# The head of a hybrid attention and state-space block, reordered

## The chip, the cores and the metric

One core of a Trainium2 chip runs the whole program in one launch. The metric is the device time of that launch in microseconds (us), lower is better. The engines of the core are TensorE (PE in the profile, with its weight loads PEld), VectorE (DVE), ScalarE (ACT), GpSimd (POOL) and SyncE (SP), which only issues transfers here. Each takes its instructions strictly in the order of its own queue and waits there for what the next instruction needs.

## What is computed

The reference is a streaming-encoder block on 1040 rows (16 meta tokens and 1024 tokens) of width 1024, all in float32. Cut to what this case needs:

```
xn   = rmsnorm(concat(meta, x), g)
q, k, v, f, u, gates = split(xn @ w_in)
y_a  = forgetting_attention(q, k, v, f) @ w_attn_out
z    = gelu(s5(u))                 # diagonal state-space model, 32 groups x 64 states
zg   = z @ w_glu
y_s  = zg[:, :1024] * sigmoid(zg[:, 1024:])
g    = sigmoid(gates)
h    = h + (g[:, :1024] * y_a + g[:, 1024:] * y_s) @ w_o
h    = h + (silu(gate) * val) @ w_down    # val, gate = causal conv of rmsnorm(h) @ w_up
out  = rmsnorm(h)[16:]

s5:  lam_bar = exp(lam * dt), dt = exp(log_dt), b_bar = (lam_bar - 1) / lam * b
     state_t = lam_bar * state_(t-1) + b_bar u_t;  y_t = Re(c state_t) + d u_t
```

## The kernel before

Activations are held by features: xhi and xlo are two tiles [128, 8, 1040] whose sum is the normalised input, a rounded part and the rest. Weights are split the same way (whi, wlo). A product of such pairs is three matmuls for each slice of 128 features (L146, L147, L148 in `dense_steps`): hi by hi, hi by lo, lo by hi.

The head, which is what the change touches, does the following.

- The meta tile (`xm`, 16 rows) and eight token tiles (`xt`, 128 rows) are loaded. `norm_rows` squares one on ScalarE (L161), turns the sum into mean plus epsilon on VectorE (`vr`, L163), takes the power -0.5 on GpSimd (`rs`, L165) and scales the tile by it and by the gain `g1B` on VectorE (L166).
- `to_feature` transposes the scaled tile in two halves of four 128x128 pieces on TensorE (L175), copies each half to xhi on ScalarE (L177) and writes the rest to xlo on VectorE (L126).
- `u_weights(m)` splits the weights of column chunk m (0 to 3) of the state-space input: a copy on ScalarE (L281) and a subtraction on VectorE (L126). `u_proj(0)` multiplies chunks 0 and 1 and `u_proj(2)` chunks 2 and 3, each over three blocks of 272, 384 and 384 rows (24 matmuls a block and chunk), and writes u to DRAM.
- `ssm(...)` builds the state-space model. Its first step, the discretisation, is a long row of small VectorE operations on tiles of 128x32 (`sm`), from log dt and lambda to the powers of lam_bar. `tables(q)` then makes Gm, Kt, Vm and Wi for a quarter of the groups (TensorE at L1495 and L1515), and `chain(q)` the recurrence (L1532, L1572).
- Between those, `gate_chunk(i)` for i = 8 to 15 multiplies the second half of the gates. Its weights come by `wchunk` with `act` and `adds` set: a load on GpSimd's queue (L130), a rounded copy on ScalarE (L134), the negative raw weights on ScalarE (L138), and a second, accumulating load that adds the raw weights' bits (L139), which leaves raw minus rounded in `wlo`.
- After the gates come the first pair of q and k (`project_qk`), the forget gate, and `load_z` with the glu.

The buffers `raw`, `whi` and `wlo` exist twice, so a new weight chunk waits until the matmuls of the last but one are done. In the head the same `raw` slots hold two of the four u weight tiles.

The order within each engine's queue comes from a scheduler that simulates the program; `after(a, b)` adds a rule of order by hand that a comes after b. In what follows names with a number (sm_155, whi_951) are single buffers of that name.

## Time and profile before

| what | value |
|---|---|
| time, median of three runs (lowest to highest) | 1498.87 us (1498.07 to 1501.14) |
| the profiled execution, its own time | 1501.19 us |
| span of that execution, first to last instruction | 1499.4 us |
| mean granted clock of TensorE | 0.992 |
| busy: PE, DVE, ACT, POOL | 1452.1, 1067.2, 678.4, 656.9 us |
| chain that ended last, by engine | PE 78%, DVE 12%, DMA 4%, issue 3% |
| transfers | 187.81 MB, mean 125 GB/s |

Rows of the profile are read so: a group or an instruction shows its line, engine and operation, then written tile and read tiles with partitions x elements, then its time, and in brackets how long the engine idled before it and what released it. A row of a stretch shows the stretch, its length, the busy time and number of instructions of each engine, the granted clock of TensorE (1.00 is full), the share of the transfer engines and GB/s. A row of waits shows who waited for what: us in total, how often, longest. The chain of waits is the work that ended last, followed back from release to release.

### The profile page before, as it was taken

The page shows a single profiled execution, that of the slowest core. Times are in us where ns is not written, and L with a number is a line of the kernel's source. Part 1 is how long each engine was busy: PE and PEld are TensorE (multiplying, and loading weights), DVE is VectorE, ACT ScalarE, POOL GpSimd, SP SyncE. Part 2 cuts the span into 40 slices and gives each one's busy share as a digit, 9 for nine tenths or more (in the row PEclk, how much of TensorE's full clock was granted, in tenths as well). Part 3 has the DMA queues.
Part 4 walks back from the last instruction along what each step waited for, and adds up shares of the span by engine and source line. Part 5 has one row for each costly group of instructions (what it writes and reads, how often), then busy time and mean ns, then how long its engine had stood idle before and what let it go on. Part 6 is the DMA issues. An engine that isn't in the chain of part 4 may idle for free.

```text
span 1499.4 us, 26213 instructions
## 1 busy us (share of the span) xinstructions
PE 1452.1 (97%) x9637; PEld 1364.1 (91%) x9637; DVE 1067.2 (71%) x2259; ACT 678.4 (45%) x1321; POOL 656.9 (44%) x743
## 2 busy tenths in 40 slices
PE   5999999999999999999999999999999999989997
PEld 4999999998999999999778999999999999768886
DVE  7989568862657676656255988887787776688785
ACT  6255565532646565532033534444444445444433
POOL 2010004750655556525010235555544326689765
PEclk9999999999999999999999999999999999999998
DMA  5365553550121212157241226776643215864413
GB/s 214 87 151 150 128 142 100 166 160 30 33 79 40 79 32 83 43 185 269 84 158 68 71 86 168 198 193 186 158 115 96 74 60 177 320 214 125 143 36 113
DMA packets 82837, 187.81 MB, mean 125 GB/s; under 512 B 13610, under 2 KB 26554, under 8 KB 82356
## 3 DMA queue, kind: packets, MB, share of 16 engines
q1 hardware_dynamic: 68212, 155.56, 31.8%
q0 software_dynamic: 8704, 19.98, 7.4%
q10 hardware_dynamic: 5792, 10.60, 1.9%
q8 instruction: 76, 1.25, 0.4%
q14 instruction: 53, 0.43, 0.1%
HBM read 146.98 MB, written 61.00 MB: 139 GB/s over the span
## 4 chain that ended last, share of the span: by engine, by line
PE 78%; DVE 12%; DMA 4%; issue 3%; ACT 2%; POOL 1%; SPq 0%; POOLq 0%; DVEq 0%; ACTq 0%
PE mm L148 5%; PE mm L146 5%; PE mm L147 5%; PE sp L203 4%; PE sp L204 4%; PE sp L205 4%; PE tp L203 3%; PE tp L204 3%; PE tp L205 3%; PE tp L685 2%; PE mm L203 2%; PE mm L205 2%; PE mm L204 2%; PE po L707 2%; PE po L706 2%
## 5 line engine op out<-in xcount | busy, mean ns | idle before, releaser
L148 PE MATMUL mm<-xhi,wlo 128*128 128x342 f32 (+2 forms) x584 | 191.0, 328 | 2.3 <-DMA wlo<-in_w_g_dram 2.3
L146 PE MATMUL mm<-xhi,whi 128*128 128x342 f32 (+2 forms) x584 | 191.9, 329 | 1.0 <-DVE q L126 1.0
L147 PE MATMUL mm<-xlo,whi 128*128 128x342 f32 (+2 forms) x584 | 190.8, 327 | 1.4 <-DVE xlo L126 1.4
L148 PEld LDWEIGHTS mm<-xhi,wlo 128*128 128x128 f32 x584 | 111.5, 191 | 3.1 <-DMA wlo<-in_w_g_dram 2.5
L146 PEld LDWEIGHTS mm<-xhi,whi 128*128 128x128 f32 x584 | 111.8, 192 | 2.1 <-PE sp L643 0.8
L147 PEld LDWEIGHTS mm<-xlo,whi 128*128 128x128 f32 x584 | 111.8, 191 | 2.1 <-DVE xlo L126 1.7
L126 DVE TENSOR_TENSOR sw<-sf,sw 128x512 fp32r<-128x512 f32 x76 | 72.5, 955 | 48.6 <-ACT sw L937 48.5
L968 POOL TENSOR_TENSOR ov<-ov,og 128x1024 f32<-128x1024 f32 x21 | 51.4, 2449 | 120.6 <-ACT og L967 117.7
L937 ACT CAST sw<-sf 128x512 fp32r<-128x512 f32 x76 | 47.4, 624 | 113.4 <-POOL sf L945 86.0
L945 POOL TENSOR_TENSOR sf<-raw,sf 128x512 f32<-128x512 f32 x38 | 64.9, 1709 | 69.1 <-DVE sw L126 68.8
L205 PE MATMUL mm<-xhi,sw 128*128 128x256 f32 (+1 forms) x304 | 85.5, 281 | 0.0
L203 PE MATMUL mm<-xhi,sw 128*128 128x256 f32 (+1 forms) x304 | 85.4, 281 | 0.1
L204 PE MATMUL mm<-xlo,sw 128*128 128x256 f32 (+1 forms) x304 | 85.2, 280 | 0.0
L692 ACT CAST th<-tp 128x256 fp32r<-128x256 f32 (+3 forms) x120 | 56.1, 472 | 61.6 <-PE tp L685 28.6
L126 DVE TENSOR_TENSOR tl<-tp,th 128x256 fp32r<-128x256 f32 (+3 forms) x120 | 65.2, 547 | 26.1 <-ACT th L692 24.7
L937 ACT CAST sw<-raw 128x512 fp32r<-128x512 f32 x69 | 42.4, 620 | 83.3 <-DMA raw<-in_w_up_dram 36.4
L657 POOL TENSOR_SCALAR pt<-pt,nm 128x144 f32<-128x144 f32 (+4 forms) x72 | 50.9, 708 | 52.3 <-DVE nm L656 51.0
L945 POOL TENSOR_TENSOR sf<-raw 128x512 f32<-128x512 f32 x38 | 50.5, 1329 | 52.0 <-DMA raw<-in_w_up_dram 24.8
L1034 DVE SCALAR_TENSOR_TENSOR ov<-hv,cwt,ov 128x1024 f32<-128x1024 f32 x38 | 72.9, 1919 | 0.4 <-ACT ov L1032 0.4
L655 ACT ACTIVATE pt<-pt,nm 128x144 f32<-128x144 f32 (+4 forms) x72 | 52.9, 735 | 26.2 <-DVE nm L654 25.8
L648 DVE CUSTOM_DVE_ANT_0 pt<-sp,fb 128x328 f32<-128x328 f32 (+8 forms) x112 | 46.4, 430 | 20.6 <-PE sp L643 12.3
L165 POOL TENSOR_TENSOR rs<-vr,nhalf 128x1 f32<-128x1 f32 (+2 forms) x18 | 10.5, 592 | 109.5 <-PE mm L889 52.4
(606 smaller groups left out, 5417.9 us busy)
## 6 DMA issues: line engine op xcount, KB each, us to landing
raw<-in_w_up_dram SPq DMA_DIRECT2D x44, 512.0 KB, 3.7
t_d<-in_w_dn_dram POOLq DMA_DIRECT2D x44, 256.0 KB, 6.9
ar<-a_d SPq DMA_DIRECT2D x44, 256.0 KB, 4.9
wr<-t_d SPq DMA_DIRECT2D x44, 256.0 KB, 3.1
a_d<-ov SPq DMA_DIRECT2D x21, 512.0 KB, 2.6
wr<-in_w_dn_dram SPq DMA_DIRECT2D x33, 256.0 KB, 3.5
t_d<-in_w_dn_dram SPq DMA_DIRECT2D x22, 256.0 KB, 4.4
t_d<-t_d SPq DMA_DIRECT2D x22, 256.0 KB, 4.5
```

The source lines that it names most:

```text
L126: return eng.tensor_tensor(out_, src, hi.bitcast(F), ALU.subtract)
L146: yield PE.matmul(ps, whi[:, i, :], ahi[:, i], start=(i == 0), stop=False)
L147: yield PE.matmul(ps, whi[:, i, :], alo[:, i], start=False, stop=False)
L148: yield PE.matmul(ps, wlo[:, i, :], ahi[:, i], start=False, stop=(i == k - 1))
L203: PE.matmul(ps, a[0][:, i], bh, start=(i == 0 and not joins), stop=False, skip_group_check=True)
L204: PE.matmul(ps, a[0][:, i], bl, start=False, stop=False, skip_group_check=True)
L205: PE.matmul(ps, a[1][:, i], bh, start=False, stop=(i == kh - 1), skip_group_check=True)
L655: S.activation(pt[:n, :kc], pt[:n, :kc], AF.Exp, bias=nm[:n, 1:2], scale=0.125, accum_out=nm[:n, 2:3])
L692: S.copy(th[:kn, z:tw], tp[:kn, z:tw])
L937: S.copy(hi, src)
L945: sums.append(GP.tensor_tensor(f_, a, b, op))
L1034: V.scalar_tensor_tensor(out=o, in0=h_[:, j:SEQ + j], scalar=cwc(j, m), in1=o, op0=ALU.mult, op1=ALU.add)
```

## The change

It does ten things, nine of them in the head.

1. `u_weights` takes its weights by column chunks: the array `w_u` is laid out in blocks, one 512 KB tile for each chunk m instead of one for each two slices of features. A chunk is split with two copies and two subtractions of 128x512 instead of four and four of 128x256. Chunk 0 is split ahead of token tile 2 and chunk 1 ahead of token tile 3 (tile 0 is the meta tile) instead of before all tiles.
2. The loads of SP's queue stand in another order: `g1B` first (it was on ScalarE's queue), and the four u chunks between the token tiles.
3. The discretisation starts behind the scaling of the fifth tile (`scales[4]`) instead of before the tiles.
4. It is shorter: polynomials take one operation a step instead of two (`horner`), complex products work on both parts in one tile (`cmul`), and the powers are built as unit numbers E and radii rp.
5. From token tile 3 on, the squares of a tile come after the xhi copies of the tile two before (`done[i - 2]`), where only tile 3 came after the copies of the tiles before it.
6. 20 transposes of the identity stand at the head of TensorE's queue (L299).
7. `u_proj(2)` goes through all blocks of chunk 2 and then all of chunk 3; before, the two alternated by block, as they still do in `u_proj(0)`.
8. `wchunk` loads on GpSimd's queue where `act` is set, which now includes the first q and k weights.
9. Four of the 32 z loads (m = 3, odd g) go to GpSimd's queue.
10. `norm_rows` returns its scaling instruction as well, for point 3.

The diff, with the discretisation cut to its core:

```diff
-        (GP if adds else SY).dma_start(raw, src)
+        (GP if act else SY).dma_start(raw, src)
...
-    uraw = [wp.tile([P, 2, SW], F, tag="raw", name="uraw") for _ in range(2)]
-    uraw += [sp.tile([P, 2, SW], F, tag="Tm", name="uraw", bufs=2) for _ in range(2)]
+    uraw = [wp.tile([P, KD, P], F, tag="raw", name="uraw") for _ in range(2)]
+    uraw += [sp.tile([P, KD, P], F, tag="Tm", name="uraw", bufs=2) for _ in range(2)]
...
-        for j, raw in enumerate(uraw):
-            src, sl = raw[:, :, P * m:P * m + P], slice(2 * j, 2 * j + 2)
-            S.copy(hi[:, sl], src)
-            split_lo(V, lo[:, sl], src, hi[:, sl])
+        for j in range(2):
+            sl = slice(4 * j, 4 * j + 4)
+            S.copy(hi[:, sl], uraw[m][:, sl])
+            split_lo(V, lo[:, sl], uraw[m][:, sl], hi[:, sl])
...
-    S.dma_start(g1B, g1.partition_broadcast(P))
+    SY.dma_start(g1B, g1.partition_broadcast(P))
...
-        if i == 1:
-            for j, raw in enumerate(uraw):
-                SY.dma_start(raw, w_u[:, 2 * j:2 * j + 2])
+        if i in (1, 2, 4, 6):
+            m = (1, 2, 4, 6).index(i)
+            SY.dma_start(uraw[m], w_u[m])
     ssm_loads()
-    next(ssm_steps)
-    for m in range(2):
-        u_weights(m)
-    done = []
+    warm = po_ps()
+    for _ in range(20):
+        PE.transpose(warm[:, :P], ident, ident)
+    done, scales = [], []
...
     for i, (t, n) in enumerate(TILES):
+        if i == 2:
+            u_weights(0)
+        elif i == 3:
+            u_weights(1)
+        elif i == 6:
+            next(ssm_steps)
+            for op in ssm_log:
+                after(op, scales[4])
         xt = xts[i - 1] if i else xm
-        sq_ = norm_rows(n1, xt[:n], n, g1B, xt, sq1)
-        if i == 3:
-            for cp_ in done:
+        sq_, scaled = norm_rows(n1, xt[:n], n, g1B, xt, sq1)
+        scales.append(scaled)
+        if i >= 3:
+            for cp_ in done[i - 2]:
                 after(sq_, cp_)
-        done += to_feature(xt, n, xhi, xlo, t, rot)
+        done.append(to_feature(xt, n, xhi, xlo, t, rot))
...
-        for t, n in BLK:
-            for m in (m0, m0 + 1):
-                ps = mm_ps()
+        order = [(b, m) for b in BLK for m in (m0, m0 + 1)]
+        for (t, n), m in order if m0 == 0 else sorted(order, key=lambda o: o[1]):
+            ps = mm_ps()
...
-                SY.dma_start(zt[GC * g:GC * g + GC], ym[g])
+                (GP if m == 3 and g % 2 else SY).dma_start(zt[GC * g:GC * g + GC], ym[g])
...
-        def poly(o, z, cs):
-            TS(o, z, cs[0], cs[1], ALU.mult, ALU.add)
-            for c in cs[2:]:
-                TT(o, o, z, ALU.mult)
-                TS(o, o, c, None, ALU.add)
+        def STT(o, a, c, b, op0, op1):
+            log.append(V.scalar_tensor_tensor(out=o, in0=a, scalar=c, in1=b, op0=op0, op1=op1))
+
+        def horner(o, z, cs):
+            TS(o, z, cs[0], None, ALU.mult)
+            for c in cs[1:]:
+                STT(o, o, c, z, ALU.add, ALU.mult)
...
-        def cmul(or_, oi, ar, ai, br, bi, t, u):
-            TT(t, ar, br, ALU.mult)
-            TT(u, ai, bi, ALU.mult)
-            TT(t, t, u, ALU.subtract)
-            TT(u, ar, bi, ALU.mult)
-            TT(oi, ai, br, ALU.mult)
-            TT(oi, oi, u, ALU.add)
-            V.tensor_copy(or_, t)
+        def cmul(o, a, br, bi, t, u):
+
+            TT(t, a, br, ALU.mult)
+            TT(u, a, bi, ALU.mult)
+            TT(o[:, 0], t[:, 0], u[:, 1], ALU.subtract)
+            TT(o[:, 1], t[:, 1], u[:, 0], ALU.add)
...
+        for q in (1, 2, 4):
+            TT(rp[:, q:2 * q], rp[:, :q], rp[:, q - 1:q].broadcast_to([P, q, G]), ALU.mult)
+            cmul(E[:, :, q:2 * q], E[:, :, :q], *(both(E[:, c, q - 1:q].broadcast_to([P, q, G]), q) for c in range(2)),
+                 w1[:, :, :q], w2[:, :, :q])
...
+        TT(pr[:, 1:], rp, E[:, 0], ALU.mult)
+        TT(pi[:, 1:], rp, E[:, 1], ALU.mult)
```

What stands where in the queues changes at three places on which the prediction rests.

**VectorE, the head of its queue.** `sm` tiles are the discretisation's. Before, from the first of its operations to the scaling of the first token tile:

```order
L1243 TENSOR_SCALAR sm_155<-sm_118 128x32
L1243 TENSOR_SCALAR sm_155<-sm_155 128x32 x2
L1301 SCALAR_TENSOR_TENSOR sm_156<-sm_155,sm_118 128x32
L1243 TENSOR_SCALAR sm_158<-sm_155 128x32
L163 TENSOR_SCALAR vr<-ss 16x1
L1302 SCALAR_TENSOR_TENSOR sm_156<-sm_155,sm_156 128x32
L1243 TENSOR_SCALAR sm_157<-sm_156 128x32
L1246 TENSOR_TENSOR sm_157<-sm_157,sm_156 128x32
L1243 TENSOR_SCALAR sm_157<-sm_157 128x32
L163 TENSOR_SCALAR vr<-ss 128x1
```

and in the changed kernel, from the same place:

```order
L163 TENSOR_SCALAR vr<-ss 16x1
L166 SCALAR_TENSOR_TENSOR xm<-xm,rs,g1B 16x1024
L163 TENSOR_SCALAR vr<-ss 128x1
L166 SCALAR_TENSOR_TENSOR xt<-xt,rs,g1B 128x1024
L163 TENSOR_SCALAR vr<-ss 128x1
L126 TENSOR_TENSOR xlo<-sp,xhi 128x4x16
L126 TENSOR_TENSOR wlo<-uraw,whi 128x512 x2
L166 SCALAR_TENSOR_TENSOR xt<-xt,rs,g1B 128x1024
L126 TENSOR_TENSOR xlo<-tp,xhi 128x4x16
L126 TENSOR_TENSOR xlo<-sp,xhi 128x4x128
```

The tiles' own work now comes first; the first operation on log dt (sm_118) stands behind the fifth scaling. From the start of this place to the last tile's split there are 71 operations of the discretisation in the old queue and 80 in the new one; from there to the subtraction that completes the first table Gm the old one has 122 instructions and the new one 64.

**ScalarE, the weights of the first gate chunk.** The copies of u_proj(2) to `usb`, Kt's copies, and the gate's whi and wlo. Before:

```order
L324 COPY usb_1007<-mm_1071 128x8x48
L324 COPY usb_1018<-mm_1097 128x8x48
L1497 COPY Kt_854<-sp_855 16x512
L1497 COPY Kt_854<-tp_861 16x512
L134 CAST whi_1577<-raw_1575 128x1024
L324 COPY usb_1007<-mm_1123 128x8x48
L138 ACTIVATE wlo_1578<-raw_1575 128x1024
L1516 COPY Wi_883<-sp_884 128x512
```

and now:

```order
L333 COPY usb_957<-po_991 128x8x48
L134 CAST whi_1523<-raw_1521 128x1024
L333 COPY usb_957<-mm_1017 128x8x48
L138 ACTIVATE wlo_1524<-raw_1521 128x1024
L1497 COPY Kt_808<-sp_809 16x512
L1497 COPY Kt_808<-tp_815 16x512
L333 COPY usb_964<-mm_1043 128x8x34
L333 COPY usb_964<-mm_1069 128x8x48
```

The gate's weights moved from behind four of the six u copies (the second step behind five) to behind two (and three), that is to the end of chunk 2, with all of chunk 3 (usb_964) behind it.

**GpSimd, the gate loads.** Before, from the meta tile's power on:

```order
L165 TENSOR_TENSOR rs<-vr,nhalf 16x1
L165 TENSOR_TENSOR rs<-vr,nhalf 128x1 x6
L1428 MEMSET psn 128x8
L165 TENSOR_TENSOR rs<-vr,nhalf 128x1 x2
L1427 MEMSET pc 128x8
L1519 MEMSET dt_896 128x4
L130 DMA raw<-in_w_g_dram 128x1024 x2
```

and now:

```order
L165 TENSOR_TENSOR rs<-vr,nhalf 16x1
L165 TENSOR_TENSOR rs<-vr,nhalf 128x1 x2
L130 DMA raw<-in_w_g_dram 128x1024
L165 TENSOR_TENSOR rs<-vr,nhalf 128x1
L130 DMA raw<-in_w_g_dram 128x1024
L165 TENSOR_TENSOR rs<-vr,nhalf 128x1 x4
L1428 MEMSET psn 128x8
```

The first two gate loads, which came behind all nine powers, now stand between the second, third and fourth token tile's, since the first two u chunks leave their `raw` slots early.

More of the change, by code (lines that the diff above doesn't have):

```diff
@@ L319, in u_proj @@
             us[m] = sp.tile([P, CH, NCH], F, tag="usb", name="usb", bufs=2)
-        for t, n in BLK:
-            for m in (m0, m0 + 1):
-                ps = mm_ps()
-                dense(ps[:, :n], *uc[m], xhi[:, :, t:t + n], xlo[:, :, t:t + n], KD)
-                S.copy(us[m][:, :, t // CH:(t + n) // CH], ps[:, :n].rearrange("p (n j) -> p j n", j=CH))
+        order = [(b, m) for b in BLK for m in (m0, m0 + 1)]
+        for (t, n), m in order if m0 == 0 else sorted(order, key=lambda o: o[1]):
+            ps = mm_ps()
+            dense(ps[:, :n], *uc[m], xhi[:, :, t:t + n], xlo[:, :, t:t + n], KD)
+            S.copy(us[m][:, :, t // CH:(t + n) // CH], ps[:, :n].rearrange("p (n j) -> p j n", j=CH))
         for m in (m0, m0 + 1):
@@ L1338, in rest @@
         TT(z, r, r, ALU.mult)
-        sn, cs, t1, t2 = sm(W), sm(W), sm(W), sm(W)
-        poly(sn, z, [1 / 362880, -1 / 5040, 1 / 120, -1 / 6])
-        TT(sn, sn, z, ALU.mult)
-        TT(sn, sn, r, ALU.mult)
-        TT(sn, sn, r, ALU.add)
-        poly(cs, z, [-1 / 3628800, 1 / 40320, -1 / 720, 1 / 24, -0.5])
-        TT(cs, cs, z, ALU.mult)
+        t1, t2 = sm(W), sm(W)
+        ec = sm([P, 2, G])
+        cs, sn = ec[:, 0], ec[:, 1]
+        horner(sn, z, [1 / 362880, -1 / 5040, 1 / 120, -1 / 6])
+        STT(sn, sn, 1.0, r, ALU.add, ALU.mult)
+        horner(cs, z, [-1 / 3628800, 1 / 40320, -1 / 720, 1 / 24, -0.5])
         TS(cs, cs, 1.0, None, ALU.add)
@@ L1357, in rest, with both @@
         TS(sk, sk, -1.0, 1.0, ALU.mult, ALU.add)
-        er, ei = sm(W), sm(W)
-        cmul(er, ei, cs, sn, ck, sk, t1, t2)
+        E = big("wr", [P, 2, CH, G], "E")
+        w1, w2 = (big(n, [P, 2, 4, G], n) for n in ("ta", "tb"))
+        def both(t_, n):
+            return t_.unsqueeze(1).broadcast_to([P, 2, n, G])
+        cmul(E[:, :, 0], ec, *(t_.unsqueeze(1).broadcast_to([P, 2, G]) for t_ in (ck, sk)), w1[:, :, 0], w2[:, :, 0])
+        rp = big("wi", [P, CH, G], "rp")
+        V.tensor_copy(rp[:, 0], rad)
+        for q in (1, 2, 4):
+            TT(rp[:, q:2 * q], rp[:, :q], rp[:, q - 1:q].broadcast_to([P, q, G]), ALU.mult)
+            cmul(E[:, :, q:2 * q], E[:, :, :q], *(both(E[:, c, q - 1:q].broadcast_to([P, q, G]), q) for c in range(2)),
+                 w1[:, :, :q], w2[:, :, :q])
         pr, pi = sm([P, CH + 1, G]), sm([P, CH + 1, G])
@@ L1376, in rest @@
             S.copy(qi[:, j], pi[:, CH - 1 - j])
-        r8 = sm(W)
-        TT(r8, rad, rad, ALU.mult)
-        TT(r8, r8, r8, ALU.mult)
-        TT(r8, r8, r8, ALU.mult)
-        for _ in range(3):
-            cmul(er, ei, er, ei, er, ei, t1, t2)
         den, fr, fi = sm(W), sm(W), sm(W)
@@ L1416, in rest @@
             TT(br, xq, yq, ALU.subtract)
-            TT(xq, ar, ai, ALU.mult)
-            TT(bi, xq, xq, ALU.add)
+            STT(bi, ar, 2.0, ai, ALU.mult, ALU.mult)
         NH = NP_ // 2
```

26 lines of the change are left out of this document (8 added, 18 removed).

## The prediction

> **What bounds the kernel now.** I read the page first, then a table of stretches, then the waits of TensorE, then the stretches in which it waits, instruction by instruction.
>
> ```profile
> PE 1452.1 (97%) x9637; PEld 1364.1 (91%) x9637; DVE 1067.2 (71%) x2259; ACT 678.4 (45%) x1321; POOL 656.9 (44%) x743
> ```
>
> ```profile
> core 0: us, PE busy (x) PEld busy (x) DVE busy (x) ACT busy (x) POOL busy (x), PEclk, DMA share, GB/s
> 0.00:12.70 12.70, 0.00 (x0) 0.00 (x0) 3.81 (x25) 5.77 (x11) 3.40 (x12) 1.00 0.83 272
> 12.70:43.30 30.60, 25.71 (x149) 23.72 (x150) 29.01 (x101) 19.12 (x39) 4.62 (x9) 0.94 0.37 149
> 43.30:54.90 11.60, 11.60 (x68) 11.60 (x67) 11.40 (x69) 4.14 (x20) 0.10 (x1) 1.00 0.05 8
> 83.70:86.02 2.32, 0.05 (x1) 0.00 (x0) 1.65 (x9) 2.21 (x7) 1.32 (x2) 1.00 1.06 345
> 86.02:89.75 3.73, 3.69 (x14) 3.69 (x15) 2.95 (x4) 0.25 (x1) 0.00 (x0) 0.54 1.06 248
> 89.75:231.00 141.25, 140.81 (x966) 138.59 (x965) 103.24 (x169) 78.81 (x128) 8.24 (x14) 1.00 0.52 133
> 240.00:1499.00 1259.00, 1233.54 (x8207) 1152.24 (x8205) 879.65 (x1757) 551.16 (x1081) 633.09 (x697) 0.99 0.40 123
> ```
>
> TensorE is full nearly everywhere. So what the head loses, the end loses: from 89.75 on its queue stands almost without a gap, and the order of work from the z loads onward is the same in both kernels. The losses that the change can reach lie before 90 us: 12.7 us without work, a stretch to 43.3 that is busy only in part and partly at a low clock, a hole of 2.3 us at 83.7, and 3.7 us behind it at a granted clock of 0.54. The two longest waits of TensorE (the others are of 1.4 us and less):
>
> ```profile
> PE sp L175 <- DVE xm L166: 12.7, 1, 12.7
> PE mm L148 <- DMA wlo<-in_w_g_dram: 2.3, 1, 2.3
> ```
>
> Why the first is so long stands on VectorE, ScalarE and GpSimd:
>
> ```profile
> 4.70 1.05 ACT L161 ACTIVATE sq<-xm 16x1024 bf16<-16x1024 f32 x1 [1.42 <-DMA xm<-in_meta_dram]
> 5.66 0.18 ACT L161 ACTIVATION_READ_ACCUMULATOR sq<-xm 16x1 f32 x1
> 9.03 0.61 DVE L1243 TENSOR_SCALAR sm<-sm 128x32 f32<-128x32 f32 x3 [7.65 <-DMA sm<-in_l_dt_dram]
> 10.09 0.56 POOL L165 TENSOR_TENSOR rs<-vr,nhalf 16x1 f32<-16x1 f32 x1 [6.90 <-DVE vr L163]
> 11.38 1.27 DVE L166 SCALAR_TENSOR_TENSOR xm<-xm,rs,g1B 16x1024 f32<-16x1024 f32 x1
> ```
>
> The meta tile's squares are summed at 5.84, but VectorE's queue has the first operation of the discretisation ahead of them, and that waits for log dt until 9.03. Behind it, small operations and tile work alternate.
>
> **The change part by part.** The profiled execution took 1501.19 us, a hair above the three timed runs (1498.07 to 1501.14), and 2.3 us above their median of 1498.87. Its span is 1499.4, so 1.8 us lie around it. The terms below are taken out of that execution and applied to the median.
>
> *First term: the end of the first projection, u_proj(0).* The chunks m=0 and 1 are 144 matmuls, six groups of 24. TensorE's price for them, and for the transposes:
>
> ```profile
> 17.57 1.06 PE L175 MATMUL sp<-ident,xt 128*128 128x128 f32 x4
> 21.07 0.43 PE L148 MATMUL mm<-xhi,wlo 128*128 128x272 f32 x1
> 21.30 0.43 PE L146 MATMUL mm<-xhi,whi 128*128 128x272 f32 x1
> 25.05 0.29 PE L148 MATMUL mm<-xhi,wlo 128*128 128x272 f32 x1
> 25.17 0.29 PE L147 MATMUL mm<-xlo,whi 128*128 128x272 f32 x1
> 39.85 0.44 PE tp L175 x4
> 43.20 0.34 PE L147 MATMUL po<-xlo,whi 128*128 128x384 f32 x1
> 43.38 0.34 PE L148 MATMUL po<-xhi,wlo 128*128 128x384 f32 x1
> ```
>
> From start to start a 272-wide one takes 0.23 us early and 0.125 from 25 us on; a 384-wide one takes 0.175, a transpose 0.11 (four in 0.44). When VectorE hands over the last tile's second half (43.2 us), 68 matmuls are left until 54.9. Of these, 48 are the last block, which needs that half: 48 x 0.174 = 8.35 us. The other 20 (3.5 us) are arrears. What was done from 12.7 to 43.3 would at full rate be 72 transposes (7.9), 48 x 0.125 = 6.0 and 28 x 0.174 = 4.9, so 18.8 us in 30.6, a rate of 61%.
>
> Afterwards the meta tile no longer waits for log dt: sum at 5.84, 0.15 for L163, 0.56 for the power, some 0.15 between engines, then 1.27 of scaling, gives 7.97 instead of 12.65, if g1B is there; it is now the first load of SP's queue, ahead of the first token tile, which so comes somewhat later. So TensorE can start 4.7 us sooner. It then has 18.8 + 3.5 = 22.3 us of work before the last block, which at the same 61% takes 36.6: 8.0 + 36.6 = 44.6.
>
> Is the last tile ready by then? VectorE:
>
> ```profile
> 9.03:43.30 34.27, 25.71 (x149) 23.72 (x150) 32.40 (x116) 20.98 (x43) 5.73 (x11) 0.95 0.44 178
> 44.89 0.19 DVE L1246 TENSOR_TENSOR sm<-sm,sm 128x32 f32<-128x32 f32 x1
> 44.99 0.19 DVE L1246 TENSOR_TENSOR sm<-sm 128x32 f32<-128x32 f32 x1
> 9.48 1.06 ACT L161 ACTIVATE sq<-xt 128x1024 bf16<-128x1024 f32 x1 [2.46 <-DMA xt<-in_x_dram]
> ```
>
> It was busy for 32.4 of 34.27 us. By the order of rows, 71 discretisation operations stood ahead of that last split, and now 80; nine more at 0.10 are +0.9 us. The u splits are 4 of 128x512 instead of 8 of 128x256, about 0.3 less. That makes 33.0 us from 5.9, or 38.9 without a wait. Now nothing fills the waits ahead of the fifth scaling: the second token tile lands at 9.4 (the row at 9.48), its scaling cannot begin before 9.4 + 1.25 + 0.15 + 0.56 = 11.4, and VectorE has two scalings and some 0.3 us besides to do until then, so about 2.6 us idle; two or three turns over GpSimd's power at 0.7 come on top. That gives about 43, as before. The start is sooner and the last tile is not; the gain is in the arrears. u_proj(0) ends at 44.6 + 8.35 = 52.9, I say **-2.0 us**. The bounds: -4.7 if TensorE's whole earlier start comes through, 0 if nothing does.
>
> The 20 warm-up transposes lie before the meta tile and cost nothing there. I take their gain as nothing too: the last of 24 transposes of the first tiles, at 17.57, still took 1.06 us for four, and the matmuls behind them went at half rate at 21.3. The Trainium skill ("TensorE: Matmul & The Clock Gate", Part 4: PE-mode transpose) says that transpose mode does not count as busy for the clock gate; the trace agrees. By it, the warm-up would bring 0; were it wrong, the term would be the second rival's.
>
> *Second term: the hole at 83.7.* It is the first gate chunk's low weights:
>
> ```profile
> 75.80 1.05 ACT L134 CAST whi<-raw 128x1024 fp32r<-128x1024 f32 x1 [2.95 <-PE mm L147]
> 77.12 1.06 ACT L138 ACTIVATE wlo<-raw 128x1024 fp32r<-128x1024 f32 x1
> 78.49 0.91 POOL L139 DMA_DIRECT2D wlo<-in_w_g_dram  x1 [19.00 <-ACT wlo L138]
> 86.06 0.45 PE L148 MATMUL mm<-xhi,wlo 128*128 128x342 f32 x1 [2.31 <-DMA wlo<-in_w_g_dram]
> ```
>
> The copy at 75.80 waits for a matmul of u_proj(2), since both chunks' weights are held until their last group. The changed order finishes m=2 first, 72 matmuls (11.35 us) after u_proj(0): 52.9 + 11.4 = 64.3. The same steps to the issue (2.7) and to landing (7.5) give 74.5; TensorE needs the weights 26 us behind u_proj(0), at 81 in the old count and 79 in the new. Spare: 4 us. **-2.3.** The second gate chunk then waits for m=3's weights, free at 79: 79 + 2.7 + 7.5 = 89, against a need at 79 + 72 x 0.155 = 90 and the state-space products between; that is close, and a rival.
>
> *Third term: the clock behind the hole.* 3.73 us at 0.54 lose 0.46 x 3.73 = **-1.7**. Without the hole I take this as gone; bounds 0 and -1.7.
>
> *The shorter discretisation* moves little on TensorE: its first table product is there in time.
>
> ```profile
> 64.85 1.35 DVE L1246 TENSOR_TENSOR Gm<-Gm,tm 128x1152 f32<-128x1152 f32 x1
> 70.31 1.05 PE L1495 MATMUL sp<-Gm,sm 128*16 128x128 f32 x8
> ```
>
> Before, the table was ready 4.1 us ahead of need. Between the last tile's split and that table VectorE had 122 instructions and now has 64; 58 at 0.10 to 0.2 are 6 to 11 us sooner. Late start, then, and no later end. Taken as 0, bounded below by 0 and above by the slower rival.
>
> *Queues.* SP gives up three kinds of issues; GpSimd takes them, behind its accumulating loads.
>
> ```profile
> 183.20 0.34 SPq L130 DMA_DIRECT2D raw<-in_w_k_dram  x1
> 183.64 26.35 SPq L471 DMA_DIRECT2D zt<-y_d  x32
> 231.80 0.36 PE L440 MATMUL po<-xhi,wf 128*64 128x384 f32 x1 [1.24 <-DVE kl L126]
> ```
>
> The k weights are loaded at 183 and multiplied long after, so waiting behind one accumulating load more on GpSimd's queue does not matter. The z loads take 26 us of issue; four of the 32 move, 3.3 us, which could let VectorE be done with z before kl at 231.8: between 0 and -1.2, taken as 0, because VectorE is then still full.
>
> Sum: -2.0 - 2.3 - 1.7 = -6.0. **1498.87 - 6.0 = 1492.9 us**; its own range, from the bounds of the terms (-8.7 and -2.3), is 1490.2 to 1496.6.
>
> **The rivals.**
>
> *The head is no sooner* (chance 0.20). The gate loads now start in the head, ahead of later tiles:
>
> ```profile
> 56.28 1.14 POOL L130 DMA_DIRECT2D raw<-in_w_g_dram  x2 [9.03 <-DVE sm L1321]
> 12.70:20.70 8.00, 5.64 (x27) 4.59 (x27) 7.90 (x23) 5.92 (x15) 1.11 (x1) 1.00 1.03 417
> 20.70:24.90 4.20, 4.20 (x18) 4.20 (x19) 3.96 (x13) 4.11 (x8) 1.07 (x2) 1.00 0.70 284
> ```
>
> These are 1 MB at 417 GB/s, 2.5 us, in a stretch where the transfer engines are full. The last tile is then handed over at 45.5 and u_proj(0) ends at 54; the gain is 4.9 us, or 3.2 where the clock's 1.7 does not come back, so 1494.0 to 1495.7; with the arrears unchanged as well, -2.3 and 1496.6. Against it: in that stretch VectorE was busy for 7.90 of 8.00 us, so it was not the tiles that came late. The Trainium skill ("DMA: Bandwidth & Descriptors", Issuing engines are not separate DMA queues) says that loads of several engines interleave on the same 16 DMA engines, so another queue saves only issue time; the full share of 1.03 agrees.
>
> *More than forecast* (0.13): the warm-up does keep the clock up. From 12.7 to 24.9 TensorE was busy for 5.6 + 4.2 = 9.8 us at half rate (the two rows above), so up to 4.9 of it could go; I hold it to the 4.7 that is the first term's bound, and with 1.2 at 231.8 that gives -4.7 - 4.0 - 1.2 = -9.9, 1489.
>
> *The hole only moves* to the second gate chunk (0.09): -2.0, perhaps less, 1496.9.
>
> *Slower* (0.08): one loop. Each tile's squares from the third on now wait for the copies of the tile two before, and those copies wait for transposes that stand in TensorE's queue behind matmuls, which wait for VectorE. One turn is 0.6 + 1.25 + 0.15 + 0.56 + 1.28 + 1.06 + 0.6 = 5.5 us for two tiles against VectorE's own 2 x 3.6; with a group of 24 half-rate matmuls (5.5 us) between it is 11 and decides. Three such turns add 11.4 us; the last tile comes at 54.6, u_proj(0) ends at 63, and with the other two terms still gained the time is +4.1, 1503. It is slower at all from a last tile at 50.6 on, and by 3 us from 53.6. Against it: one to two matmul groups were already interleaved without that.
>
> **How the numbers follow.** The forecast has 0.50, the rivals 0.20, 0.13, 0.09 and 0.08. A measurement of this kernel can tell about 0.2%, 3 us. Faster holds all of the forecast and of the second rival and just over half of the first (0.11): 0.74. Within 0.2%: the rest of the first, and the moved hole: 0.18. Slower: 0.08. The range runs from 1489 to 1497.5: it cuts the slower rival and the edges.
>
> **What would show it.** Right: meta transposes at about 8 us, the last block's end near 53, no wait for wlo of w_g, a clock of 1.00 from 80 to 91, VectorE's Gm well ahead of L1495, and the same distance between kernels at 240 us as at the end. Wrong: a last tile after 46, a wait at the second gate chunk, waits of the power on GpSimd behind its loads, or a shift that is lost again after 240 us.

## The result, and the profile after

The changed kernel takes 1488.14 us (median of four runs, 1487.17 to 1489.73), the kernel before 1499.16 (four runs beside them, 1498.07 to 1501.14). The ratio is 0.9933, with a 95% interval of 0.9917 to 0.9949: 11.0 us less. That is faster, as forecast, but almost twice the 6.0 us forecast, and 0.9 us below the lower end of the range (1489).

The profiled execution of the changed kernel took 1488.39 us, span 1486.6. The page's first part and the table of stretches, with the columns of the prediction's table (stretch, length, busy time and instructions of PE, PEld, DVE, ACT and POOL, granted clock, DMA share, GB/s):

```profile
PE 1452.2 (98%) x9657; PEld 1364.3 (92%) x9657; DVE 1066.5 (72%) x2194; ACT 675.2 (45%) x1313; POOL 657.7 (44%) x749
...
0.00:12.70 12.70, 6.42 (x36) 5.73 (x36) 4.98 (x17) 7.18 (x15) 3.95 (x13) 0.95 0.87 278
12.70:43.30 30.60, 26.12 (x155) 24.04 (x155) 28.75 (x109) 16.31 (x33) 5.12 (x10) 0.85 0.45 181
43.30:54.90 11.60, 11.60 (x70) 11.60 (x71) 11.45 (x46) 4.82 (x20) 1.06 (x2) 1.00 0.21 36
54.90:83.70 28.80, 28.80 (x193) 27.99 (x191) 25.95 (x84) 12.65 (x23) 3.87 (x5) 1.00 0.68 141
83.70:89.75 6.05, 6.05 (x44) 5.70 (x42) 6.02 (x9) 2.18 (x5) 0.00 (x0) 1.00 0.84 228
...
215.00:232.00 17.00, 16.48 (x106) 14.72 (x105) 15.26 (x31) 12.63 (x31) 1.64 (x2) 1.00 0.09 32
```

TensorE's busy time has not changed (1452.1 and 1452.2 us), so the span became shorter by idle time and low clock alone. The hole at 83.7 and the low clock behind it are gone. The clock of the stretch from 12.7 to 43.3 (0.85 here, 0.94 in the prediction's table) must not be compared: the profile has no record of the clock before its first step, at 24.89 in the kernel before and at 8.10 here, and counts that time as full, though products went at half pace there (the prediction's rows at 21.07 and 21.30). TensorE's longest waits:

```profile
PE mm L1165 <- DVE hs L1172: 3.2, 2, 1.9
PE po L299 <- POOL psn L1428: 3.2, 1, 3.2
PE tp L1165 <- DVE hs L1172: 2.7, 2, 2.3
PE sp L175 <- DVE xt L166: 2.7, 2, 2.0
PE tp L175 <- DVE xt L166: 2.3, 1, 2.3
```

No wait for wlo is left. The 12.7 us for the meta tile have become 3.2 us for GpSimd, which makes the identity that the 20 transposes need (e1 has the same wait under the identity's name), and 5 us for the scalings of the first token tiles. Single rows of the changed kernel, from the timeline:

```profile
3.16 4.53 PE L299 MATMUL po<-ident 128*128 128x128 f32 x20 [3.16 <-POOL psn L1428]
7.64 0.59 PE L175 MATMUL sp<-ident,xm 16*128 16x16 f32 x4
10.44 0.66 PE L175 MATMUL sp<-ident,xt 128*128 128x128 f32 x4 [1.96 <-DVE xt L166]
42.47 0.61 PE L146 MATMUL mm<-xhi,whi 128*128 128x384 f32 x2 [0.24 <-ACT xhi L177]
43.71 0.69 DVE L126 TENSOR_TENSOR xlo<-sp,xhi 128x512 fp32r<-128x512 f32 x1
51.23 0.34 PE L148 MATMUL mm<-xhi,wlo 128*128 128x384 f32 x1
59.55 1.34 DVE L1255 TENSOR_TENSOR Gm<-Gm,tm 128x1152 f32<-128x1152 f32 x1
64.42 0.39 PE L1495 MATMUL sp<-Gm,sm 128*16 128x128 f32 x2
65.54 0.92 POOL L139 DMA_DIRECT2D wlo<-in_w_g_dram  x1 [9.61 <-PE sp L1495]
172.39 25.40 SPq L480 DMA_DIRECT2D zt<-y_d  x28
221.18 0.31 PE L449 MATMUL mm<-xhi,wf 128*64 128x272 f32 x1 [0.40 <-DVE q L126]
221.74 0.69 DVE L126 TENSOR_TENSOR zlo<-zf,zhi 128x520 fp32r<-128x520 f32 x1
```

The last product of u_proj(0) in the kernel before:

```profile
54.92 0.34 PE L148 MATMUL mm<-xhi,wlo 128*128 128x384 f32 x1
```

u_proj(0) has 144 products, and the rows at 51.23 and 54.92 are the 144th in each kernel; the next ones (128x272, at 51.41 and 55.10) open u_proj(2). The last token tile's last split is done 1.1 us later than before (43.71 + 0.69 = 44.40 for 43.30), and u_proj(0) still ends 3.7 us sooner: its arrears are gone. Behind that split 39 products are left, where the kernel before has 67. The accumulating load of the first gate chunk's low weights is issued at 65.54 instead of 78.49.

**Where the time went.** I paired the same TensorE instruction in both traces and took the difference of its starts, so each figure says how much sooner the changed kernel is at that place (in the time of the kernel before):

| place | sooner by, us | step | forecast of the step |
|---|---|---|---|
| end of u_proj(0) (54.9) | 3.7 | -3.7 | -2.0 |
| first matmul of gate chunk 8 (80.9) | 3.6 | +0.1 | 0 |
| its product behind the hole (86.1) | 6.3 | -2.7 | -2.3 |
| 200 | 7.8 | -1.5 | -1.7 |
| 240 | 9.0 | -1.2 | 0 |
| 765 | 8.6 | +0.4 | 0 |
| 775 | 10.1 | -1.5 | 0 |
| 1000 | 11.5 | -1.4 | 0 |
| 1480 | 11.0 | +0.5 | 0 |
| end of the span (1499.4) | 12.8 | -1.8 | 0 |

Around 86 us the two queues do not hold the same order, so only the sum of the steps to 86.1 and to 200 (-4.2) is firm. The profiled execution of before was 2.0 us above its median, that of the changed kernel 0.3, so these traces differ by 12.8 us in span where the medians differ by 11.0. The later steps must be read with that in mind. The second executions of both kernels (e9 and e10, below), paired in the same way, repeat some steps and not others: 3.5 at the end of u_proj(0), and -1.4 near 775; but +0.9 between 200 and 240, where the table has -1.2.

### The profile page after: what moved, and what is told of

Read it like the earlier page. It is cut to its first block, busy times and chain, and to the rows that moved or that the text cites. A ratio compares the mean times of both kernels' runs of the same rounds, so it can differ in the third digit from the quotient of the medians.

```text
span 1486.6 us, 26188 instructions
## 1 busy us (share of the span) xinstructions
PE 1452.2 (98%) x9657; PEld 1364.3 (92%) x9657; DVE 1066.5 (72%) x2194; ACT 675.2 (45%) x1313; POOL 657.7 (44%) x749
## 4 chain that ended last, share of the span: by engine, by line
PE 81%; DVE 11%; issue 2%; ACT 2%; DMA 2%; POOL 1%; SPq 0%; DVEq 0%; POOLq 0%; ACTq 0%
PE mm L148 5%; PE mm L147 5%; PE mm L146 5%; PE sp L203 4%; PE sp L204 4%; PE sp L205 4%; PE tp L203 3%; PE tp L204 3%; PE tp L205 3%; PE tp L694 3%; PE mm L205 2%; PE mm L203 2%; PE mm L204 2%; PE po L716 2%; PE po L715 2%
## 5 line engine op out<-in xcount | busy, mean ns | idle before, releaser
L126 DVE TENSOR_TENSOR sw<-sf,sw 128x512 fp32r<-128x512 f32 x76 | 74.7, 982 | 49.7 <-ACT sw L946 49.7
L126 DVE TENSOR_TENSOR tl<-tp,th 128x256 fp32r<-128x256 f32 (+3 forms) x120 | 65.1, 547 | 25.8 <-ACT th L701 24.5
```

The source lines that it names most:

```text
L126: return eng.tensor_tensor(out_, src, hi.bitcast(F), ALU.subtract)
```

## The experiments

Theory A is the forecast's reading: the gain is made in the head, by VectorE doing the tiles' own work first and by the chunk order of u_proj(2), which closes the hole and with it the low clock behind it; the warm-up, the queues and the shorter discretisation add nothing. The rivals put the gain, or a part of it, elsewhere: in the warm-up's clock, in where the loads are issued, in fewer operations of VectorE, or in nothing but the scatter between executions. Letters in an expectation stand for the theories as that expectation states them. "Shift" is the paired difference as above, + where the kernel is later than the one it is set against; "lost at the forget gate" is the shift that arises between 200 and 240 us, where q and k are split on VectorE (L126) and the forget gate (L449) follows.

| run | median, us (lowest to highest) | before beside it | ratio to before (95%) | gain, us |
|---|---|---|---|---|
| changed kernel | 1488.14 (1487.17 to 1489.73) | 1499.16 | 0.9933 (0.9917 to 0.9949) | 11.0 |
| e1, u_proj(2) alternates | 1493.52 (1490.79 to 1494.02) | 1498.76 | 0.9963 (0.9951 to 0.9974) | 5.2 |
| e2, before with chunk order | 1495.87 (1493.46 to 1498.89) | 1498.76 | 0.9979 (0.9969 to 0.9989) | 2.9 |
| e3, discretisation first | 1499.10 (1496.75 to 1503.02) | 1498.76 | 1.0008 (0.9998 to 1.0018) | -0.3 |
| e4, no warm-up | 1490.50 (1489.54 to 1492.99) | 1498.76 | 0.9948 (0.9936 to 0.9960) | 8.3 |
| e5, discretisation last | 1495.61 (1493.50 to 1496.34) | 1499.22 | 0.9973 (0.9962 to 0.9985) | 3.6 |
| e6, long discretisation | 1490.15 (1489.58 to 1492.48) | 1499.22 | 0.9940 (0.9928 to 0.9953) | 9.1 |
| e7, g1B on ScalarE's queue | 1489.47 (1489.00 to 1491.65) | 1499.22 | 0.9935 (0.9923 to 0.9948) | 9.8 |
| e8, queues as before | 1489.31 (1487.10 to 1489.59) | 1499.22 | 0.9924 (0.9911 to 0.9938) | 9.9 |
| e11, more warm-up | 1491.89 (1489.55 to 1494.07) | 1499.09 | 0.9948 (0.9930 to 0.9965) | 7.2 |
| e12, before with short discretisation | 1497.01 (1492.60 to 1498.89) | 1499.09 | 0.9980 (0.9970 to 0.9991) | 2.1 |

### e1: u_proj(2) alternates again, in the changed kernel

```diff
-        for (t, n), m in order if m0 == 0 else sorted(order, key=lambda o: o[1]):
+        for (t, n), m in order:
```

> The changed kernel with u_proj(2) alternating its two chunks by block again (point 7 undone). Theory A, that the hole at 83.7 was closed by finishing chunk 2 first: both chunks' weights are again held to their last group, the accumulating load is issued about 76 instead of 66, TensorE waits some 2 to 3 us for wlo at L148 and runs some 3.4 us at half clock behind it; +4.0 us against the changed kernel, about 1492.1. Rival B, that it was closed by the gate weights' raw loads now lying in the head: no such wait, within 0.7 us of the changed kernel, about 1488.

The gain falls from 11.0 to 5.2 us. The waits of TensorE, and the stretch behind the wait for wlo:

```profile
PE mm L146 <- DVE q L126: 2.9, 3, 1.9
...
PE mm L148 <- DMA wlo<-in_w_g_dram: 2.0, 1, 2.0
```

```profile
83.58:87.00 3.42, 3.42 (x14) 3.42 (x13) 3.42 (x5) 0.00 (x0) 0.00 (x0) 0.50 1.07 245
```

Hole and half clock are back: 2.0 us, and 3.42 us at half rate, which cost 1.7. Against the changed kernel the shift is +0.3 at the end of u_proj(0) and +4.1 at 200, so 3.8 us arise between, close to the 4.0 forecast for the second and third terms together. A further 2.5 us are lost at the forget gate, which A did not foresee.

### e2: the chunk order alone, in the kernel before

```diff
-        for t, n in BLK:
-            for m in (m0, m0 + 1):
-                ps = mm_ps()
+        order = [(b, m) for b in BLK for m in (m0, m0 + 1)]
+        for (t, n), m in order if m0 == 0 else sorted(order, key=lambda o: o[1]):
+            ps = mm_ps()
```

> The kernel before with u_proj(2) by chunks alone (point 7 alone). Theory A: the hole and the low clock behind it are gone, -4.0 us against the kernel before, about 1495.2, and TensorE's first matmuls stay where they were (18.4 us). Rival B: the raw loads still start at 56, so the hole stays; within 0.7 us, about 1499.

A gain of 2.9 us, and in the trace a shift of -3.8 at 200 us and -3.1 at 240 against the kernel before. There is no wait for wlo and no low clock at 86. So this one line of the change is worth 3 to 4 us by the traces up to 200 us in either kernel, and 2.9 in the time of the kernel before.

### e3: the discretisation ahead of the tiles, in the changed kernel

```diff
+    next(ssm_steps)
     done, scales = [], []
...
-        elif i == 6:
-            next(ssm_steps)
-            for op in ssm_log:
-                after(op, scales[4])
```

> The changed kernel with the (shorter) discretisation started before the tiles again, without the rule that ties it to the fifth scaling (point 3 undone). Theory A, that the head gained from the tiles' own work coming first: VectorE waits for log dt until 9.0 again, the meta tile's transposes start at about 12 instead of 7.6, u_proj(0) ends 2 to 4 us later, about 1490 to 1492. Rival B, that the head is bounded by VectorE's total up to the last tile's split, which is the same set of operations: last split at 43 to 44 in both, no difference within 0.7 us, about 1488.

The whole gain is undone. TensorE's waits and two rows of VectorE:

```profile
PE sp L175 <- DVE vr L163: 3.9, 2, 2.8
PE sp L175 <- DVE xm L166: 3.8, 1, 3.8
...
PE po L148 <- DVE wlo L126: 2.1, 1, 2.1
```

```profile
8.46 0.61 DVE L1249 TENSOR_SCALAR sm<-sm 128x32 f32<-128x32 f32 x3 [7.08 <-DMA sm<-in_l_dt_dram]
...
10.12 1.27 DVE L166 SCALAR_TENSOR_TENSOR xm<-xm,rs,g1B 16x1024 f32<-16x1024 f32 x1
```

VectorE again idles 7.08 us for log dt with the meta tile's sum waiting behind it, and the small operations again stand between the tiles. The last split comes 6.8 us later than in the changed kernel and the end of u_proj(0) 6.7, which is later than in the kernel before as well (57.94 for 54.92); that the u splits and the squares tied to earlier copies now stand behind the delay is my reading of it, not tested apart. At 200 us it is still 6.7 behind the changed kernel, at 240 it is 10.7: the wait of 2.1 us for VectorE's split of a weight lies between, and a half clock from 219.2 to 222.6. So without the order of VectorE's queue the rest of the change brings nothing, and a part of that is again lost behind 200 us. The forecast of this run was too small, like the forecast of the change.

### e4 and e11: without the warm-up, and with more of it

```diff
-    warm = po_ps()
-    for _ in range(20):
-        PE.transpose(warm[:, :P], ident, ident)
```

> The changed kernel without the 20 transposes of the identity (point 6 undone). Theory A, that they bring nothing: within 0.7 us, about 1488, although the first token tile's transposes, which took 0.6 us for four at 10.4, may take 1.1 again. Rival B, that they raise the clock early and the head lives on it: later by 1.5 to 4.7 us, 1489.6 to 1492.8.

e11 keeps the 20 transposes and puts 10 more behind the meta tile's and 12 more behind the first token tile's:

```diff
         done.append(to_feature(xt, n, xhi, xlo, t, rot))
+        for _ in range((10, 12)[i] if i < 2 else 0):
+            after(PE.transpose(warm[:, :P], ident, ident), last_tr[0])
```

> The changed kernel with 10 and 12 more transposes of the identity behind the meta tile's and the first token tile's transposes, so that TensorE has work until the second token tile. Theory A, that VectorE's own work (busy 28.75 of 30.6 us to 43.3) bounds the last split: the clock is at 1.00 from about 8 to 12 us on, first matmuls at 0.125 apiece instead of 0.23, but u_proj(0) ends only 0 to 1.5 us sooner; 1486.6 to 1488.2. Rival B, that the half rate up to 21.75 is paid in full: 3 to 4 us sooner, 1484 to 1485. Rival C: transposes do not keep the clock up at all: the rise stays at 22 to 23 us, 1488 to 1489.

A row of e4's timeline:

```profile
10.68 1.12 PE L175 MATMUL sp<-ident,xt 128*128 128x128 f32 x4 [1.80 <-DVE xt L166]
```

and of e11's:

```profile
12.41 1.48 PE L321 MATMUL mm<-ident 128*128 128x128 f32 x12
13.98 0.65 PE L177 MATMUL tp<-ident,xt 128*128 128x128 f32 x4
```

Without the warm-up the four transposes take 1.12 us instead of 0.66, so the clock is lower, and yet u_proj(0) ends at 49.96, 1.3 us sooner than in the changed kernel; 0.9 of it goes into a wait for VectorE's split of the next weights, and from 60 to 215 us the shift is -0.1. The head does not lose by it. Its median gains 2.8 us less, with intervals that overlap; that lies where rival B put the time, but the loss is not in the head, where B put it. Its profiled execution, 2.5 us above that median, loses 2.7 at the forget gate and 3.3 near 770, where it waits 1.9 for xs and has the low clock. With the longer warm-up the clock is full from 12.3 us on, 9 us sooner than in the changed kernel, and the end of u_proj(0) comes at the same time (shift -0.06).

What sets that end shows when all executions are put side by side. In the ten with the changed order of the tiles (e3 among them) the last product of u_proj(0) starts 6.7 to 7.4 us behind the end of VectorE's last split, with 39 to 42 products left; in the four with the old order it is 11.0 to 11.6 us, with 63 to 67 left. So the last split on VectorE sets the end of the head, as A claims, and the changed order takes away the arrears behind it. What sets the last split itself e4 and e11 do not show cleanly: the scheduler also changed VectorE's order in them, so that 111 and 114 of its instructions stand ahead of that split instead of 127. That e11 is then 3.8 us slower was in no expectation: its trace shows a half clock from 29.4 to 32.8, and +0.7 at 60 us, +1.8 at 240. Why the rest follows stays open.

### e5: the discretisation behind the ninth scaling instead of the fifth

```diff
-        elif i == 6:
-            next(ssm_steps)
-            for op in ssm_log:
-                after(op, scales[4])
...
+    next(ssm_steps)
+    for op in ssm_log:
+        after(op, scales[8])
```

> The changed kernel with the discretisation put behind the ninth tile's scaling instead of the fifth's (point 3 carried further). Theory A, that u_proj(0) of the changed kernel is bounded by VectorE's last split (44.3 us, then 8.35 us of last block), and that the 80 small operations in front of it are what is left to take away: last split at about 36 instead of 43.7, u_proj(0) ends 3 to 5 us sooner (47 to 49), the first table still ready before its need; 1483.5 to 1485.5. Rival B, that TensorE's own work and its low clock until 22 us set the end, or that the tables come late: same time or later, 1488 to 1492.

The gain shrinks to 3.6 us. By stretches, by TensorE's waits from 200 to 240, and by the timeline:

```profile
12.70:43.30 30.60, 27.32 (x161) 25.43 (x162) 23.80 (x55) 16.62 (x33) 5.57 (x10) 1.00 0.45 182
...
54.90:83.70 28.80, 28.80 (x185) 28.15 (x184) 28.40 (x106) 12.28 (x30) 2.92 (x4) 1.00 0.68 147
...
215.00:232.00 17.00, 12.50 (x66) 10.74 (x65) 16.71 (x28) 11.55 (x26) 0.00 (x0) 0.90 0.00 0
```

```profile
PE mm L448 <- DVE q L126: 2.9, 1, 2.9
PE mm L203 <- DVE fl__2548 L451: 1.0, 1, 1.0
PE mm L146 <- DVE q L126: 0.9, 1, 0.9
PE mm L203 <- DVE kl L126: 0.8, 1, 0.8
PE mm L448 <- DVE kl L126: 0.7, 1, 0.7
```

```profile
42.03 0.69 DVE L126 TENSOR_TENSOR xlo<-sp,xhi 128x512 fp32r<-128x512 f32 x1
...
189.90 18.24 SPq L479 DMA_DIRECT2D zt<-y_d  x28
```

In the tiles' stretch VectorE now works only 23.80 of 30.60 us, and the last split is 1.7 us sooner. VectorE has 5 us less to do there, and most of it turns into waits, the longest of them 2.82 us for ScalarE's xhi copy, at 23.9; I read this as the loop through TensorE and ScalarE taking over. A's 36 for the last split was far off. The head gains 1.1 us by it (shift -1.1 up to 215). What was pushed back fills VectorE from 54.9 to 83.7, the z loads begin at 189.9 instead of 172.4, and 8.1 us are lost from 215 to 240.

### e6: the long discretisation, in the changed kernel's order

```diff
-        def horner(o, z, cs):
-            TS(o, z, cs[0], None, ALU.mult)
-            for c in cs[1:]:
-                STT(o, o, c, z, ALU.add, ALU.mult)
+        def poly(o, z, cs):
+            TS(o, z, cs[0], cs[1], ALU.mult, ALU.add)
+            for c in cs[2:]:
+                TT(o, o, z, ALU.mult)
+                TS(o, o, c, None, ALU.add)
...
```

> The changed kernel with the longer discretisation of before (point 4 undone), still behind the fifth scaling. Theory A, that the shortening is not what made the gain: the first table Gm comes some 5 to 8 us later than the changed kernel's 51, at 56 to 59, TensorE needs it at 63; within 0.7 us, about 1488. Rival B, that the tables or the state-space chain come late without it: a wait of TensorE at the first table or at the gates around it, 1.5 to 6 us later.

The table of stretches, TensorE's waits from 200 to 240, and the timeline:

```profile
54.90:83.70 28.80, 28.80 (x186) 28.14 (x185) 28.49 (x117) 10.50 (x16) 2.92 (x4) 1.00 0.68 147
...
215.00:232.00 17.00, 12.74 (x77) 10.73 (x75) 16.75 (x29) 10.75 (x25) 0.00 (x0) 1.00 0.00 0
```

```profile
PE po L449 <- DVE kl L126: 2.6, 1, 2.6
PE mm L449 <- DVE kl L126: 1.0, 1, 1.0
PE mm L449 <- DVE q L126: 0.6, 1, 0.6
```

```profile
64.85 1.37 DVE L1255 TENSOR_TENSOR Gm<-Gm,tm 128x1152 f32<-128x1152 f32 x1
...
178.61 26.51 SPq L480 DMA_DIRECT2D zt<-y_d  x28
...
229.59 0.69 DVE L126 TENSOR_TENSOR zlo<-zf,zhi 128x520 fp32r<-128x520 f32 x1
```

The last step of the first table Gm comes 5.3 us later (64.85 for 59.55; the 51 of the expectation was too early), and no wait of TensorE arises there: up to 215 us the shift is -0.8 (15 fewer VectorE instructions stand ahead of the last split). But VectorE is busy 28.49 of 28.80 us behind the tiles, where the short one leaves it 2.85 free. The z loads begin 6.2 us later, the last z split stands at 229.59 instead of 221.74, and 4.6 us are lost at the forget gate, in this execution. By the medians the long discretisation costs 2.0 us, by the ratios 0.07% or 1.0, with intervals that overlap; so the place is shown by the trace and the size is not settled.

### e7 and e8: the queues

```diff
-    SY.dma_start(g1B, g1.partition_broadcast(P))
+    S.dma_start(g1B, g1.partition_broadcast(P))
```

> The changed kernel with g1B loaded from ScalarE's queue behind the meta tile again (the first part of point 2 undone). Theory A, that the meta tile's early scaling needs g1B early: g1B lands at about 9 to 10 with the others, the meta transposes start at about 11 instead of 7.6, and the last split moves by part of it, +1 to +3 us, 1489 to 1491. Rival B, that the transfers share their bandwidth anyway and the start does not matter for the last split: within 0.7 us, about 1488.

```diff
-        (GP if act else SY).dma_start(raw, src)
+        (GP if adds else SY).dma_start(raw, src)
...
-                (GP if m == 3 and g % 2 else SY).dma_start(zt[GC * g:GC * g + GC], ym[g])
+                SY.dma_start(zt[GC * g:GC * g + GC], ym[g])
```

> The changed kernel with the first q and k loads and all z loads on SP's queue again (points 8 and 9 undone). Theory A, that no one waits for them: nothing in the head, at the forget gate up to the 1.2 us that the kernel before waited there; 0 to +1.2, 1488 to 1489.4. Rival B, that the gain beyond the forecast (5 us) came from these queues: +2 to +5, 1490 to 1493.

With g1B on ScalarE's queue the meta tile's scaling comes 3 us later:

```profile
PE sp L175 <- DVE xm L166: 3.9, 1, 3.9
```

but the shift in the head is only +1.4, and the time cannot be told from the changed kernel's. In e8 the shift is +0.2 to +0.5 up to 880 us, and the time cannot be told apart either.

### e9 and e10: both kernels once more

These are the two kernels without an edit, for one look each, to see which waits belong to a kernel and which to an execution.

> The kernel before once more, unchanged, for a second trace. Theory A, that the two differences behind 700 us (TensorE's wait of 1.5 us for the second norm's xs near 771, and the 6.8 instead of 3.4 us of half clock near 875) are those of an execution: at least one of them is absent or of another size here, while the waits before 90 us (12.7 and 2.3) and at 231.8 (1.2) are as before within 0.3 us. Rival B, that they belong to the kernel: both are there again.

> The changed kernel once more, unchanged, for a second trace. Theory A: TensorE stands at most 0.5 us at the forget gate near 223 and the head's end (u_proj(0) at 52.2) is the same within 1 us; the stretch of full clock from 8.1 to 11.5 us is there in one execution and not in another, since it depends on where a window falls. Rival B: waits at the forget gate vary by 1 us and more from execution to execution, so that what the variants showed there is noise.

TensorE's waits in the kernel before, again:

```profile
PE mm L148 <- DMA wlo<-in_w_g_dram: 2.8, 1, 2.8
...
PE sp L175 <- DVE xs L166: 1.4, 1, 1.4
```

The hole and the wait for xs near 775 us (L166) are in both executions of the kernel before and in neither of the changed kernel; the hole is the kernel's, and for xs this speaks for the kernel too: e2 and e12, with the old order, have it as well (1.4 and 1.8). Of the variants of the changed kernel e4 has it in full (1.9), e8 and e11 have 0.3 and 0.5, the others none. The low clock does not: the kernel before had 6.8 us of it near 875 us in the first execution and none there in the second, where instead the stretch behind the hole was 6.8 us long. The changed kernel had 3.4 us of it at 865 in the first execution and none in the second. At the forget gate the second execution of the changed kernel waited 1.7 us (q, 1.2 and 0.5) where the first waited 0.4. So some 1.4 us there are scatter; the 4.6 of e6 and the 8.1 of e5 are far beyond it, the 2.5 to 2.7 of e1, e4 and e7 only in part. A's bounds were too tight: the kernel before waited 2.8 us for wlo where it had waited 2.3, and 0.7 for kl where it had waited 1.2, and the changed kernel's 1.7 is rival B's.

### e12: the shorter discretisation alone, in the kernel before

```diff
-        def poly(o, z, cs):
-            TS(o, z, cs[0], cs[1], ALU.mult, ALU.add)
-            for c in cs[2:]:
-                TT(o, o, z, ALU.mult)
-                TS(o, o, c, None, ALU.add)
+        def horner(o, z, cs):
+            TS(o, z, cs[0], None, ALU.mult)
+            for c in cs[1:]:
+                STT(o, o, c, z, ALU.add, ALU.mult)
...
```

> The kernel before with the shorter discretisation alone (point 4 alone). Theory A, that it pays where TensorE would otherwise come to the q, k and forget products before VectorE has done z: here the hole at 83.7 and the low clock behind it stay, the 1.2 + 0.3 us at 231.8 and 238.7 go; -0.5 to -2.5 us, 1496.5 to 1498.5. Rival B, that it carries much of the whole gain by itself: -4 us or more, below 1495. Rival C: nothing, within 0.5 us.

A gain of 2.1 us, of the size expected, but not at the place. In the trace the last split comes 2.0 us and the end of u_proj(0) 2.6 us sooner, since fewer small operations stand between the tiles. The wait for wlo is 2.0 us, and no half clock follows it in this execution, so that the kernel is 4.6 us ahead at 200. At the forget gate, where A put the gain, TensorE waits 2.1 us instead of 1.5, and 0.8 us are lost.

## Why the prediction came out as it did

**What held.** The direction, and the places named: the meta tile's transposes at 7.64 (forecast 8), the last tile no sooner than before (done at 44.4, 1.1 us later; forecast "about 43, as before"), the first projection ending sooner all the same because its arrears were done, no wait for wlo, a clock of 1.00 from 80 to 91. The first term came to -3.7 for -2.0, the second and third together to -4.2 for -4.0; in all -7.9 where -6.0 was forecast. e1 shows the last two by taking them away (3.8 us in the head). The step to the issue of the low weights was right within 1.5 us (65.54 for 67).

**The rivals.** "The head is no sooner" did not come: the loads on GpSimd's queue delayed no tile. "The hole only moves" did not: the second gate chunk's weights are issued at 79.9 and TensorE does not wait. "Slower" did not: copies and squares show as a limit in e5, where VectorE has less to do, and bring no later tile there. "More than forecast" gave nearly the right time (1489) without its reason being shown: it put the gain down to the warm-up's clock, and without the warm-up u_proj(0) ended 1.3 us sooner, not later (e4).

**The term mis-sized most: the first.** It was -2.0 and came to -3.7. The forecast had TensorE done with its arrears at 44.6 and then all 48 products of the last block to do, because that block "needs that half", the last tile's second half. Measured, the block began at 42.47, and nine of its products ran before the last split was done at 44.40. Up to 42.47 TensorE had done its 22.3 us of work since 7.64, a rate of 64% where I carried over 61%; and the block took 8.8 us from its first product to its last where I had 8.35. Between u_proj(0) and the first gate matmul nothing more was gained: TensorE has the same 169 matmuls there in both kernels and does not wait.

**A step that failed: "The shorter discretisation ... Taken as 0".** I asked only whether TensorE waits for the first table product, and it does not, with the short one or the long one (e6). But in e5 and e6, where VectorE has more to do behind the tiles, the z loads start 17.5 and 6.2 us later, and so VectorE is later done with z and free to split q and k. There the forecast took "231.8" as 0, "because VectorE is then still full". Read right, that same observation was the warning: if TensorE comes forward by 7.8 us and VectorE does not, the 1.24 us wait grows. The z loads had to come forward too, and they did, by 11.2 us (183.64 to 172.39), more than TensorE's 7.8. So what was priced as a gain of 0 was, as I read it, the price of keeping the other terms; e6 puts it at 1 to 2 us, with intervals that overlap. That the step of -1.2 between 200 and 240 is its own is not shown: it lies within the scatter of 1.4, and the second executions have +0.9 there. In the kernel before, the shorter one paid in the head instead (e12). Six kernels in which TensorE is at 200 us within 1.4 us of the changed kernel, and two executions of that kernel, in order of the last split of z:

| kernel | z loads begin | last split of z (zlo<-zf) begins | TensorE's waits, 200 to 240 |
|---|---|---|---|
| changed kernel | 172.4 | 221.7 | 0.4 |
| e8 | 174.7 | 222.0 | 0.7 |
| changed kernel, e10 | 172.1 | 223.0 | 1.7 |
| e4 | 175.0 | 224.8 | 1.9 |
| e11 | 175.7 | 225.2 | 1.5 |
| e7 | 175.1 | 227.2 | 2.7 |
| e6 | 178.6 | 229.6 | 4.5 |
| e5 | 189.9 | 232.4 | 6.3 |

The later VectorE ends its work on z, the longer TensorE waits, but for e11. This is an ordering over traces; it is not an experiment on that wait alone.

**"The same distance between kernels at 240 us as at the end"** was wrong by about 2 us: 9.0 at 240 and 11.0 at 1480, with 1.8 more in the last 20 us of these executions. The 1.5 us at 775 are a wait for xs that the kernel before has in both its executions. The 1.4 between 860 and 1000 come from the low clock near 870, which differs from execution to execution (e9: -1.9 against the first execution of the same kernel). Why xs is in time in the changed kernel stays open: e4 also has that wait (1.9 us), and it has the changed order of the tiles. So of the 5.0 us beyond the forecast 1.7 are the first term's and about 1.4 the wait for xs, both found again in the second executions (1.5 and 1.4); the rest is not assigned to a place.

**"The trace agrees"** on the warm-up was a step that failed as a reading; no cost of it shows in the head, and it is told below.

Nothing that ran beats the changed kernel; e7 and e8 cannot be told from it.

## What to carry to other kernels

On engines that work in order, put what the next stage waits for at the head of the queue, and an operation that waits for a slow load behind it: taking that order away lost all 11 us here (e3). When the busiest engine comes forward, ask at each later meeting place whether its partner comes forward as much, because work that is hidden in the trace of before is the partner's slack in the trace after. And a hole is worth its length and the low clock behind it, here about 4 us together, if the same weights can be released sooner by finishing one user first.
